# Eight more weight tiles split early and kept in DRAM, with their stores one plan entry later

## The chip, the cores and the metric

The kernel runs on one core of a Trainium2 chip. The metric is the device time of one execution, in microseconds (us). The core has a matrix engine (PE, with its weight loads as PEld), a vector engine (DVE), a scalar engine (ACT), a general engine (POOL) and a queue engine that issues the DMAs (SP). Each engine works through its own instructions in the order in which they were emitted; semaphores tie them to each other.

## The reference, cut to what matters

Two layers of a streaming encoder on a sequence of 512 rows with 1024 features. Layer 0 mixes with gated linear attention, layer 1 with chunked softmax attention; each layer then has a feed-forward block of width 4096. All weights are float32.

```python
def reference(x, c, w_ada, ...):
    c_act = jax.nn.silu(c)
    for i in range(DEPTH):                      # DEPTH = 2
        mods = jnp.split(c_act @ w_ada[i] + b_ada[i], 6, axis=-1)
        sh1, sc1, g1, sh2, sc2, g2 = [m[:, None, :] for m in mods]
        u = x * (1.0 + sc1) + sh1
        y = gla_mixer(u, ...) if i % 2 == 0 else chunk_attention(u, ...)
        x = layer_norm(ALPHA * x + (1.0 + g1) * y, ...)
        u = x * (1.0 + sc2) + sh2
        y = jnp.square(jax.nn.relu(u @ ff_w1[i])) @ ff_w2[i]
        x = layer_norm(ALPHA * x + (1.0 + g2) * y, ...)
    return x
```

`chunk_attention` has 16 heads; its input projections are `u @ att_w_in` (queries, keys, values) and its output projection is `o @ att_w_out`.

## The kernel before, in words

Activations lie feature by row, so a matmul's moving operand is a 128 x 512 tile of activations and its stationary operand a 128 x 128 block of weights. A **unit** is a weight tile of 128 x 1024 (eight such blocks) and makes one output tile of 128 x 512. To keep float32 accuracy every operand is split into a high part `hi` (a cast to float32r) and a low part `lo` (the value minus `hi`), and each block is multiplied three times, hi·hi, hi·lo and lo·hi (`mm3`). A unit is thus 24 matmuls.

Splitting a weight tile takes a load into a buffer of `rawp` (five buffers, `raw`), a cast on ACT (`A.copy`) and a subtraction on DVE (`lo_of`). The two results go into the pool `wp` (tags `whi` and `wlo`, four buffers each, for units used in order) or into two buffers of the pool `act` (26 buffers, shared with the activations; named `fhi` and `flo`).

What is loaded and split when is set by a list, `plan`, that is written before the program: `emit_unit` takes the next entry and emits its instructions. The kinds are `"w"` (load a unit and split it into `wp`), `"f"` and `"F"` (the same into `act`, for the four tiles that open a feed-forward block), `"a"` (one eighth of one modulation vector: load a tile, one DVE instruction on it), `"c"` (load a tile, split it into `act`, and store both parts to DRAM, "keep" it), and `"x"` and `"X"` (load a kept tile's two parts from DRAM straight into `wp` or `act`, with no cast and no subtraction). `next_w` hands out the next unit and then calls `fill`, which emits plan entries until three units are ready ahead. ACT and DVE run in the order of emission (`InOrder`); the DMAs are issued by SP in an order that the framework's scheduler chooses, and a DMA that waits holds up those behind it.

The feed-forward block of layer 0 (`add_mlp(0, ...)`) has 48 entries for units in its main loop, each with an `"a"` entry, and among them 18 `"c"` entries: the 14 query and key tiles of layer 1 from the second on (`kqk`), and tiles 0 to 3 of the output projection (`a_o`). Layer 1's attention takes them back as `"x"` and `"X"`. Its last four output-projection tiles are `"w"` entries, and the four tiles that open layer 1's feed-forward block are `"f"` and `"F"` entries; both are loaded and split while attention ends.

After attention comes `boundary(..., late=True)`: the output projection's tiles 0 to 3 over all rows (with the last heads' work between them, functions `t1` to `t5`), a matmul whose ACT copy gives `shift`, then `fill_f(4)`, then `sub` and `start_acc` (DVE and ACT) while PE does tiles 4 to 7 on the first half of the rows and tile 4 on the second half, then `stats1`, whose matmuls (`ones_c`) read the sums that DVE accumulates, and then the normalised tiles `un`, which PE takes half by half (`fg`). The boundary after layer 0's attention runs the same code from `stats1` on, `fg` included.

Of the kernel before, what the change touches and what calls it, by code (L numbers as in the profile page):

```python
# [9 lines left out]
F32 = mybir.dt.float32  # L10
# [49 lines left out]
def trunk(ctx, tc, xT, c, ada, cols, gk1, gk2, w_qk, w_v, w_g, w_go, a_qk, a_v, a_tab,  # L60
          a_win, a_o, f1, f2, out):
    nc = tc.nc
# [13 lines left out]
    def nm(s):  # L76
        uid[0] += 1
        return f"{s}{uid[0]}"
# [16 lines left out]
    def lo_of(eng, o, x, hi):  # L95
        return eng.tensor_tensor(out=o, in0=x, in1=hi.bitcast(F32), op=ALU.subtract)
# [35 lines left out]
    def ada_unit(l, t, k):  # L132
        raw = rawp.tile([P, D], F32, tag="raw", name=nm("raw"))
        nc.sync.dma_start(out=raw, in_=ada[l, t * 8 + k])
        i = t * 8 + k
        V.scalar_tensor_tensor(out=raw, in0=raw, scalar=1.0, in1=csil, op0=ALU.mult, op1=ALU.mult,
                               accum_out=mods[:, l, i:i + 1])
        if t == G2:
            tt(V, mods[:, l, i:i + 1], mods[:, l, i:i + 1], col[:, C_ADA + l * 48 + i:C_ADA + l * 48 + i + 1], ALU.add)
        elif k == KT - 1:  # L140
            m8 = mods[:, l, t * 8:t * 8 + 8]
            tt(V, m8, m8, col[:, C_ADA + l * 48 + t * 8:C_ADA + l * 48 + t * 8 + 8], ALU.add)
# [35 lines left out]
    plan = []  # L178
    state = {"pos": 0, "look": 0}
    ready_w, ready_f = [], []  # L180

    kept = {}

    def split_w(in_act):
        if in_act:
            return (act.tile([P, D], F32R, tag="act", name=nm("fhi")), act.tile([P, D], F32R, tag="act", name=nm("flo")))
        return (wp.tile([P, D], F32R, tag="whi", name=nm("whi")), wp.tile([P, D], F32R, tag="wlo", name=nm("wlo")))

    def emit_unit():
        kind, what = plan[state["pos"]]  # L190
        state["pos"] += 1
        if kind == "a":
            ada_unit(*what)
            return
        if kind in "xX":
            hi, lo = split_w(kind == "X")
            nc.sync.dma_start(out=hi.bitcast(F32), in_=kept[what][0])
            nc.sync.dma_start(out=lo.bitcast(F32), in_=kept[what][1])
            ready_w.append((hi, lo))
            return  # L200
        if kind == "c":
            key, src = what
            raw = rawp.tile([P, D], F32, tag="raw", name=nm("raw"))
            nc.sync.dma_start(out=raw, in_=src)
            hi, lo = split_w(True)
            A.copy(out=hi, in_=raw)
            lo_of(V, lo, raw, hi)
            kept[key] = [dram.tile([P, D], F32, name=f"{n}_{key[0]}{key[1]}") for n in ("khi", "klo")]
            nc.sync.dma_start(out=kept[key][0], in_=hi.bitcast(F32))
            nc.sync.dma_start(out=kept[key][1], in_=lo.bitcast(F32))  # L210
            return
        raw = rawp.tile([P, D], F32, tag="raw", name=nm("raw"))
        nc.sync.dma_start(out=raw, in_=what)
        hi, lo = split_w(kind in "fF")
        A.copy(out=hi, in_=raw)
        lo_of(V, lo, raw, hi)
        (ready_f if kind in "fF" else ready_w).append((hi, lo))

    def fill(n=None):
        n = state["look"] if n is None else n  # L220
        while len(ready_w) < n and state["pos"] < len(plan):
            emit_unit()

    def fill_f(n):
        while len(ready_f) < n:
            emit_unit()
# [13 lines left out]
    def add_units(units, adas=(), per=1, kind="w"):  # L240
        adas = list(adas)
        for u in units:
            plan.append((kind, u))
            for _ in range(per):
                if adas:
                    plan.append(("a", adas.pop(0)))

    def add_out(units, fgs, adas=(), early=False, pool=0):
        adas = list(adas)
        for i, u in enumerate(units):  # L250
            plan.append(("X", ("o", i)) if early and i < 4 else ("p" if i < pool else "w", u))
            if fgs and not early and 1 < i < 6:
                plan.append(("f", fgs[i - 2]))
            if adas and i < 4:
                plan.append(("a", adas.pop(0)))
        for a in adas:
            plan.append(("a", a))
        if early:
            plan.extend(("fF"[i // 2], u) for i, u in enumerate(fgs))

    def ada_list(l, *ts):
        return [(l, t, k) for t in ts for k in range(8)]

    add_units([w_v[k] for k in range(8)], ada_list(0, G1))
    add_units([w_g[k] for k in range(8)], ada_list(0, SC2, SH2), 2)
    fg1 = lambda l: [f1[l, m] for m in range(4)]
    add_out([w_go[k] for k in range(8)], fg1(0))

    def add_mlp(l, fgs, ad, keep=()):
        ad = list(ad)  # L270
        for m in range(4, 8):
            plan.append(("p" if m < 5 else "w", f1[l, m]))
        rest = [u for g in range(3) for u in [f2[l, g * 8 + m] for m in range(8)] + [f1[l, g * 8 + 8 + m] for m in range(8)]]
        keep = list(keep)
        for i, u in enumerate(rest):
            plan.append(("w", u))
            if ad:
                plan.append(("a", ad.pop(0)))
            if keep and i % 5 in (1, 3):
                plan.append(("c", keep.pop(0)))  # L280
        assert not ad and not keep
        add_out([f2[l, 24 + m] for m in range(8)], fgs)

    kqk = [q + p for p in range(1, 8) for q in (0, 8)]
    add_mlp(0, [a_v[k] for k in range(4)], ada_list(0, G2) + ada_list(1, SH1, SC1, G1, SC2, SH2),
            [(("q", i), a_qk[i]) for i in kqk] + [(("o", i), a_o[i]) for i in range(4)])
    add_units([a_v[k] for k in range(4, 8)])
    add_units([a_qk[0], a_qk[8]])
    for i in kqk:
        plan.append(("x", ("q", i)))  # L290
    add_out([a_o[k] for k in range(8)], fg1(1), early=True)
    add_mlp(1, [], ada_list(1, G2))

    def wk(w, k, n=P):
# [12 lines left out]
    def ln_cols(l, i, nxt):  # L307
        r = {}
        g = col[:, C_LNG + (l * 2 + i) * 8:C_LNG + (l * 2 + i) * 8 + 8]
        b = col[:, C_LNB + (l * 2 + i) * 8:C_LNB + (l * 2 + i) * 8 + 8]  # L310
        r["g"], r["b"] = g, b
        if nxt is not None:
            nl, sh, sc = nxt
            mS = mods[:, nl, sc * 8:sc * 8 + 8]
            mH = mods[:, nl, sh * 8:sh * 8 + 8]
            a1 = const.tile([P, 8], F32, name=nm("a1"))
            b1 = const.tile([P, 8], F32, name=nm("b1"))
            tt(V, a1, g, mS, ALU.mult)
            tt(V, b1, b, mS, ALU.mult)
            tt(V, b1, b1, mH, ALU.add)  # L320
            ag = const.tile([P, 8], F32, name=nm("ag"))
            ab = const.tile([P, 8], F32, name=nm("ab"))
            V.tensor_scalar(out=ag, in0=g, scalar1=ALPHA, scalar2=None, op0=ALU.mult)
            V.tensor_scalar(out=ab, in0=b, scalar1=ALPHA, scalar2=None, op0=ALU.mult)
            r.update(a=a1, b1=b1, ag=ag, ab=ab)
        return r
# [877 lines left out]
    def opener(es, n):  # L1204
        def f():
            if es is not None:
                es.close()
            e = ExitStack()
            cur["es"] = e
            cur["tmp"] = e.enter_context(tc.tile_pool(name=f"lnt{n}", bufs=1))  # L1210
            return cur["tmp"]
        return f
# [4 lines left out]
    o, ev, es = gla()  # L1217
    evac_h, run = mlp_fns()
    u = boundary(o, 0, G1, opener(es, 0), lambda: ln_cols(0, 0, (0, SH2, SC2)), evac_h, ev)
    hs = run(u, 0)  # L1220
    u = boundary(hs, 0, G2, open_v, lambda: ln_cols(0, 1, (1, SH1, SC1)), None, vfill=vfill)
    cur["es"].close()
    lnc1 = ln_cols(1, 0, (1, SH2, SC2))
    o, ev, es = att(u, cur["es_v"])
    evac_h, run = mlp_fns()
    u = boundary(o, 1, G1, opener(es, 1), lambda: lnc1, evac_h, ev, late=True)
# [55 lines left out]
```

## Time and profile before

| | |
|---|---|
| median of 3 runs (lowest to highest) | 1203.96 us (1203.43 to 1204.31) |
| the profiled execution | 1204.22 us, of which the profile's span is 1202.5 us |
| PE busy | 1175.6 us, 98% |
| PEld busy | 981.6 us, 82% |
| DVE busy | 825.9 us, 69% |
| ACT busy | 555.4 us, 46% |
| HBM read and written | 174.37 MB and 20.97 MB |

The profile is of one execution. Busy times are sums over the span, so an engine with a low share can still be the one that is waited for in a stage. PE's clock has two levels, 1.2 and 2.4 GHz; the profile gives it as a fraction of the higher one. A row of the time line gives a start, a length, the instruction group, and in square brackets how long the engine was idle before it and whom it waited for.

### The profile page before, as it was taken

To read this page: it belongs to the slowest core of one execution; us is meant where nothing else is said; L and a number is where in the kernel's file an instruction comes from. 1 tells how busy PE (TensorE), PEld (TensorE's weight loads), DVE (VectorE), ACT (ScalarE), POOL (GpSimd) and SP (SyncE) were. 2 spreads that over 40 slices of the span, in tenths; PEclk is the share of its full clock that TensorE was granted. 3 is DMA by queue.
4 is the path that set the end of the run, shared out by engine and by line. 5 is a ranking of instruction groups with operands and counts; after the bars stand their busy time and mean duration, and the time that the engine had idled before them with its cause. 6 is when DMAs were issued, how large, how long until landed. Compare 5 with 4: busy or idle time off the path is not lost.

```text
span 1202.5 us, 15104 instructions
## 1 busy us (share of the span) xinstructions
PE 1175.6 (98%) x5742; PEld 981.6 (82%) x5742; DVE 825.9 (69%) x1359; ACT 555.4 (46%) x870; POOL 51.5 (4%) x61
## 2 busy tenths in 40 slices
PE   9999999999999999999999999998999999999995
PEld 5888888898888888888888787787888888888885
DVE  6789589877676677657845889987774443443467
ACT  4565555484243343343546676554742322422324
POOL 2000000000000000000011233200000000000000
PEclk9999999999999999999999999998999999999998
DMA  9756534128889889854026431440263322232302
GB/s 349 256 181 220 193 105 150 44 85 298 311 307 339 295 306 318 306 180 158 12 92 230 158 114 53 149 141 1 73 218 130 98 98 97 94 105 88 105 1 71
DMA packets 58283, 196.34 MB, mean 163 GB/s; under 512 B 6561, under 2 KB 10913, under 8 KB 58210
## 3 DMA queue, kind: packets, MB, share of 16 engines
q1 hardware_dynamic: 58210, 195.37, 46.8%
q8 instruction: 45, 0.74, 0.2%
q14 instruction: 28, 0.23, 0.1%
HBM read 174.37 MB, written 20.97 MB: 162 GB/s over the span
## 4 chain that ended last, share of the span: by engine, by line
PE 77%; DVE 14%; ACT 4%; issue 2%; POOL 1%; DMA 1%; SPq 0%; DVEq 0%; ACTq 0%; POOLq 0%
PE ps L47 77%; DVE af L47 6%; DVE x L47 4%; ACT af L47 2%; DVE wlo L47 1%; ACT ar L47 1%; POOL mb L47 1%; DVE flo L47 1%; DMA hraw<-ada 1%; ACT u L47 0%; DVE d L47 0%; DVE t L47 0%; DVE ar L47 0%; DVE y L47 0%; DVE raw L47 0%
## 5 line engine op out<-in xcount | busy, mean ns | idle before, releaser
L47 PE MATMUL ps<-ar,whi 128*128 128x512 f32 (+1 forms) x2880 | 819.8, 373 | 0.6 <-ACT ar L47 0.4
L47 PEld LDWEIGHTS ps<-ar,whi 128*128 128x128 f32 x2880 | 525.1, 189 | 96.6 <-issue 2.2
L47 PE MATMUL ps<-ar,wlo 128*128 128x512 f32 (+1 forms) x1440 | 525.2, 371 | 0.1
L47 PEld LDWEIGHTS ps<-ar,wlo 128*128 128x128 f32 x1440 | 272.3, 189 | 46.9 <-DVE wlo L47 0.8
L47 ACT CAST whi<-raw 128x1024 fp32r<-128x1024 f32 (+1 forms) x169 | 169.4, 1010 | 199.4 <-PE ps L47 163.7
L47 DVE TENSOR_TENSOR wlo<-raw,whi 128x1024 fp32r<-128x1024 f32 x162 | 197.1, 1222 | 23.2 <-ACT whi L47 21.2
L47 DVE SCALAR_TENSOR_TENSOR x<-ps,mods,x 128x512 f32<-128x512 f32 (+1 forms) x96 | 63.2, 659 | 120.2 <-PE ps L47 119.9
L47 DVE TENSOR_TENSOR h<-r 128x512 f32<-128x512 f32 (+1 forms) x72 | 45.1, 632 | 79.2 <-ACT r L47 78.3
L47 ACT ACTIVATE r<-ps 128x512 f32<-128x512 f32 (+1 forms) x72 | 38.9, 546 | 126.9 <-PE ps L47 126.9
L47 DVE SCALAR_TENSOR_TENSOR raw<-raw,csil 128x1024 f32<-128x1024 f32 x80 | 96.8, 1217 | 0.0
L47 DVE TENSOR_TENSOR ar<-h,ar 128x512 fp32r<-128x512 f32 (+1 forms) x72 | 45.5, 632 | 39.6 <-ACT ar L47 38.5
L47 PE MATMUL ps<-ar,fhi 128*128 128x256 f32 (+1 forms) x320 | 68.9, 310 | 2.3 <-DVE ar L47 2.3
L47 ACT CAST ar<-h 128x512 fp32r<-128x512 f32 (+1 forms) x72 | 41.2, 573 | 50.4 <-DVE h L47 50.4
L47 PE MATMUL ps<-whi,ar 128*128 128x512 f32 x192 | 60.7, 390 | 0.0
L47 PEld LDWEIGHTS ps<-ar,fhi 128*128 128x128 f32 x320 | 52.0, 191 | 6.5 <-DVE ar L47 3.8
L47 PE MATMUL ps<-ar,flo 128*128 128x256 f32 (+1 forms) x160 | 48.7, 305 | 0.0
L47 ACT ACTIVATE af<-x 128x256 f32<-128x256 f32 (+1 forms) x48 | 23.0, 485 | 45.6 <-DVE x L47 42.4
L47 PEld LDWEIGHTS ps<-whi,ar 128*128 128x128 f32 x192 | 36.1, 188 | 7.6
L47 ACT CAST fhi<-raw 128x1024 fp32r<-128x1024 f32 x30 | 31.1, 1048 | 22.5 <-DMA raw<-a_qk 13.2
L47 DVE TENSOR_TENSOR ar<-f,ar 64x512 fp32r<-64x512 f32 x32 | 32.2, 1005 | 12.8 <-ACT ar L47 12.2
L47 ACT ACTIVATE ar<-x,b,a 128x256 fp32r<-128x256 f32 x48 | 28.5, 594 | 25.7 <-DVE x L47 25.7
L47 POOL PARTITION_ALL_REDUCE mb<-af x16 | 33.8, 2112 | 121.2 <-DVE af L47 121.2
(141 smaller groups left out, 1024.5 us busy)
## 6 DMA issues: line engine op xcount, KB each, us to landing
raw<-f SPq DMA_DIRECT2D x128, 512.0 KB, 4.3
raw<-ada SPq DMA_DIRECT2D x80, 512.0 KB, 4.8
hraw<-ada SPq DMA_DIRECT2D x16, 512.0 KB, 9.0
raw<-a_qk SPq DMA_DIRECT2D x16, 512.0 KB, 5.3
khi_q<-fhi SPq DMA_DIRECT2D x14, 512.0 KB, 2.9
klo_q<-flo SPq DMA_DIRECT2D x14, 512.0 KB, 4.7
whi<-khi_q SPq DMA_DIRECT2D x14, 512.0 KB, 3.3
wlo<-klo_q SPq DMA_DIRECT2D x14, 512.0 KB, 4.2
```

What stands on the lines that cost most here:

```text
L47: r = f(*a, **k)
```

## The change

Eight more tiles become `"c"` entries in layer 0's feed-forward block: tiles 4 to 7 of the output projection (`a_o`) and the four tiles that open layer 1's feed-forward block (`f1[1, 0..3]`). There are now 26; they come at every second of the 48 entries in the main loop (24), and the last two stand behind the first two entries of the block's closing list (`add_out`). In layer 1 output tiles 4 to 7 are `"x"` entries (loaded from DRAM into `wp`) and the four others are of a new kind `"Y"` (loaded from DRAM into `act`). The two stores of a `"c"` entry are emitted after the next entry of the plan.

```diff
@@ emit_unit
-    kept = {}
+    kept, stores = {}, []
...
     def emit_unit():
         kind, what = plan[state["pos"]]
         state["pos"] += 1
+        late, stores[:] = stores[:], []
+        try_unit(kind, what)
+        for to, hi, lo in late:
+            nc.sync.dma_start(out=to[0], in_=hi.bitcast(F32))
+            nc.sync.dma_start(out=to[1], in_=lo.bitcast(F32))
+
+    def try_unit(kind, what):
         if kind == "a":
             ada_unit(*what)
             return
-        if kind in "xX":
-            hi, lo = split_w(kind == "X")
+        if kind in "xXY":
+            hi, lo = split_w(kind != "x")
             nc.sync.dma_start(out=hi.bitcast(F32), in_=kept[what][0])
             nc.sync.dma_start(out=lo.bitcast(F32), in_=kept[what][1])
-            ready_w.append((hi, lo))
+            (ready_f if kind == "Y" else ready_w).append((hi, lo))
             return
         if kind == "c":
...
             kept[key] = [dram.tile([P, D], F32, name=f"{n}_{key[0]}{key[1]}") for n in ("khi", "klo")]
-            nc.sync.dma_start(out=kept[key][0], in_=hi.bitcast(F32))
-            nc.sync.dma_start(out=kept[key][1], in_=lo.bitcast(F32))
+            stores.append((kept[key], hi, lo))
             return
@@ add_out
-            plan.append(("X", ("o", i)) if early and i < 4 else ("p" if i < pool else "w", u))
+            plan.append(("X" if i < 4 else "x", ("o", i)) if early else ("w", u))
+            if keep:
+                plan.append(("c", keep.pop(0)))
...
         if early:
-            plan.extend(("fF"[i // 2], u) for i, u in enumerate(fgs))
+            plan.extend(("Y", ("f", i)) for i in range(4))
@@ add_mlp
-            if keep and i % 5 in (1, 3):
+            if keep and i % 2:
                 plan.append(("c", keep.pop(0)))
-        assert not ad and not keep
-        add_out([f2[l, 24 + m] for m in range(8)], fgs)
+        assert not ad
+        add_out([f2[l, 24 + m] for m in range(8)], fgs, keep=keep)
...
-            [(("q", i), a_qk[i]) for i in kqk] + [(("o", i), a_o[i]) for i in range(4)])
+            [(("q", i), a_qk[i]) for i in kqk] + [(("o", i), a_o[i]) for i in range(8)]
+            + [(("f", i), f1[1, i]) for i in range(4)])
```

On DVE at the end of layer 1's attention, before the change: the last subtraction for an output tile (`wlo`), the last heads' result (`ar`), the four residual updates (`x_94` to `x_97` from `ps`), four subtractions for the next block's tiles (`flo`), and the first two of the `sub` group.

```order
L47 TENSOR_TENSOR wlo_6807<-raw_6804,whi_6806 128x1024
L47 SCALAR_TENSOR_TENSOR ar_6810<-af_6783,col,ar_6810 128x512
L47 SCALAR_TENSOR_TENSOR x_94<-ps_6651,mods,x_94 128x512
L47 SCALAR_TENSOR_TENSOR x_95<-ps_6703,mods,x_95 128x512
L47 SCALAR_TENSOR_TENSOR x_96<-ps_6754,mods,x_96 128x512
L47 SCALAR_TENSOR_TENSOR x_97<-ps_6822,mods,x_97 128x512
L47 TENSOR_TENSOR flo_6881<-raw_6878,fhi_6880 128x1024
L47 TENSOR_TENSOR flo_6887<-raw_6884,fhi_6886 128x1024
L47 TENSOR_TENSOR flo_6893<-raw_6890,fhi_6892 128x1024
L47 TENSOR_TENSOR flo_6899<-raw_6896,fhi_6898 128x1024
L47 TENSOR_TENSOR x_98<-x_98,af_6612 128x512
L47 TENSOR_TENSOR x_94<-x_94,af_6612 128x512
```

The same place on DVE after the change:

```order
L47 SCALAR_TENSOR_TENSOR af_6861<-ps_6856,af_6861 64x512
L47 SCALAR_TENSOR_TENSOR ar_6882<-af_6861,col,ar_6882 128x512
L47 SCALAR_TENSOR_TENSOR x_94<-ps_6731,mods,x_94 128x512
L47 SCALAR_TENSOR_TENSOR x_95<-ps_6783,mods,x_95 128x512
L47 SCALAR_TENSOR_TENSOR x_96<-ps_6832,mods,x_96 128x512
L47 SCALAR_TENSOR_TENSOR x_97<-ps_6894,mods,x_97 128x512
L47 TENSOR_TENSOR x_98<-x_98,af_6692 128x512
L47 TENSOR_TENSOR x_94<-x_94,af_6692 128x512
```

The eight subtractions of that stage (four `wlo`, of which the last is shown, and four `flo`) are gone; nothing else moved. On ACT the eight casts beside them are gone in the same way.

On SP in the second half of layer 0's feed-forward block, before the change (`raw<-f` is a unit's load, `raw<-ada` a modulation tile's, `raw<-a_o` the load of a tile to keep, `khi_o` and `klo_o` the two stores):

```order
L209 DMA khi_o_4089<-fhi_4085 128x1024
L213 DMA raw_4129<-f 128x1024
L134 DMA raw_4161<-ada 128x1024
L210 DMA klo_o_4090<-flo_4086 128x1024
L213 DMA raw_4164<-f 128x1024
L134 DMA raw_4196<-ada 128x1024
L204 DMA raw_4199<-a_o 128x1024
L213 DMA raw_4209<-f 128x1024
L134 DMA raw_4241<-ada 128x1024
L209 DMA khi_o_4205<-fhi_4201 128x1024
L213 DMA raw_4244<-f 128x1024
```

The same queue after the change:

```order
L195 DMA khi_o_4165<-fhi_4161 128x1024
L196 DMA klo_o_4166<-flo_4162 128x1024
L219 DMA raw_4204<-f 128x1024
L134 DMA raw_4236<-ada 128x1024
L211 DMA raw_4239<-a_o 128x1024
L219 DMA raw_4247<-f 128x1024
L134 DMA raw_4281<-ada 128x1024
L195 DMA khi_o_4245<-fhi_4241 128x1024
L196 DMA klo_o_4246<-flo_4242 128x1024
L219 DMA raw_4284<-f 128x1024
L134 DMA raw_4322<-ada 128x1024
```

In both, a kept tile's load, a unit's load and a modulation load stand ahead of its first store; after the change the second store follows the first at once, and the next kept tile comes sooner.

On SP late in the attention, before the change (`af<-a_win` are two heads' bias windows at a time, `fhi` and `flo` from `khi_o` and `klo_o` are output tiles 0 and 1):

```order
L986 DMA af_6305<-a_win 128x256
L986 DMA af_6308<-a_win 128x256
L986 DMA af_6468<-a_win 128x256
L986 DMA af_6471<-a_win 128x256
L197 DMA fhi_6526<-khi_o_4009 128x1024
L198 DMA flo_6527<-klo_o_4010 128x1024
L197 DMA fhi_6591<-khi_o_4089 128x1024
L198 DMA flo_6592<-klo_o_4090 128x1024
L986 DMA af_6606<-a_win 128x256
L986 DMA af_6609<-a_win 128x256
```

The same place after the change, where `whi` and `wlo` are output tiles 6 and 7 (tiles 4 and 5 stand directly ahead of the first row):

```order
L995 DMA af_6548<-a_win 128x256
L995 DMA af_6551<-a_win 128x256
L204 DMA whi_6874<-khi_o_4245 128x1024
L205 DMA wlo_6875<-klo_o_4246 128x1024
L204 DMA fhi_6606<-khi_o_3733 128x1024
L205 DMA flo_6607<-klo_o_3734 128x1024
L204 DMA whi_6878<-khi_o_4331 128x1024
L205 DMA wlo_6879<-klo_o_4332 128x1024
L204 DMA fhi_6671<-khi_o_3826 128x1024
L205 DMA flo_6672<-klo_o_3827 128x1024
L995 DMA af_6686<-a_win 128x256
L995 DMA af_6689<-a_win 128x256
```

Output tiles 4 to 7 now stand among the bias windows and tiles 0 and 1, and each waits there for a buffer of `wp`; before, their raw tiles were loaded ahead of the attention.

## Rows read from the trace of the kernel before

**Rows 1.** The page: each engine's busy time and its share of the span.
```profile
PE 1175.6 (98%) x5742; PEld 981.6 (82%) x5742; DVE 825.9 (69%) x1359; ACT 555.4 (46%) x870; POOL 51.5 (4%) x61
```

**Rows 2.** Busy time by stage, with granted clock, DMA share and GB/s last.
```profile
core 0: us, PE busy (x) PEld busy (x) DVE busy (x) ACT busy (x) POOL busy (x), PEclk, DMA share, GB/s
9.00:36.00 27.00, 26.59 (x106) 19.73 (x105) 23.92 (x40) 13.62 (x22) 5.54 (x14) 1.00 1.03 406
255.30:516.40 261.10, 261.10 (x1154) 216.24 (x1153) 185.08 (x251) 104.00 (x131) 0.00 (x0) 1.00 0.84 298
277.30:320.30 43.00, 43.00 (x192) 35.61 (x191) 30.93 (x44) 13.16 (x14) 0.00 (x0) 1.00 0.93 336
814.70:820.10 5.40, 0.00 (x1) 0.00 (x1) 4.82 (x11) 1.25 (x3) 0.00 (x0) 0.93 0.00 0
820.10:825.80 5.70, 5.70 (x22) 5.34 (x23) 4.32 (x12) 1.63 (x4) 0.00 (x0) 0.50 0.00 0
```

**Rows 3.** Time line of PE at the end of layer 1's attention and its boundary.
```profile
757.09 1.45 PE L47 MATMUL ps<-ar,ar 128*128 128x512 f32 x8
...
794.92 0.39 PE L47 MATMUL ps<-ar,flo 128*128 128x512 f32 x1
795.14 0.39 PE L47 MATMUL ps<-ar,fhi 128*128 128x512 f32 x1
796.57 0.50 PE L47 MATMUL ps<-ar,fhi 128*128 128x512 f32 x1 [1.03 <-DVE ar L47]
...
814.34 0.28 PE L47 MATMUL ps<-ar,wlo 128*128 128x256 f32 x1
820.10 0.80 PE L47 MATMUL ps<-af,ones_c 128*128 128x256 f32 x1 [5.48 <-DVE af L47]
...
842.65 0.39 PE L47 MATMUL ps<-ar,fhi 128*128 128x256 f32 x1 [0.23 <-DVE ar L47]
```

**Rows 4.** Time line of DVE in the same stage.
```profile
766.85 1.52 DVE L47 SCALAR_TENSOR_TENSOR af<-ps,ng,af 128x256 f32<-128x256 f32 x4
...
792.35 3.50 DVE L47 TENSOR_TENSOR wlo<-raw,whi 128x1024 fp32r<-128x1024 f32 x3
795.76 0.75 DVE L47 SCALAR_TENSOR_TENSOR ar<-af,col,ar 128x512 fp32r<-128x512 f32 x1
...
800.29 0.75 DVE L47 SCALAR_TENSOR_TENSOR x<-ps,mods,x 128x512 f32<-128x512 f32 x1 [0.81 <-PE ps L47]
801.15 4.63 DVE L47 TENSOR_TENSOR flo<-raw,fhi 128x1024 fp32r<-128x1024 f32 x4
805.70 3.09 DVE L47 TENSOR_TENSOR x<-x,af 128x512 f32<-128x512 f32 x5
```

**Rows 5.** Time line of ACT in the same stage.
```profile
792.36 0.72 ACT L47 ACTIVATE ar<-af,col 128x512 fp32r<-128x512 f32 x1 [0.16 <-DVE af L47]
799.59 0.60 ACT L47 ACTIVATE af<-ps 128x512 f32<-128x512 f32 x1 [6.50 <-PE ps L47]
```

**Rows 6.** Time line of PE in the boundary after layer 0's attention.
```profile
219.81 0.99 PE L47 MATMUL ps<-af,ones_c 128*128 128x256 f32 x3 [1.30 <-DVE af L47]
240.52 0.38 PE L47 MATMUL ps<-ar,fhi 128*128 128x256 f32 x1 [0.23 <-DVE ar L47]
```

**Rows 7.** Groups by line, whole run: cast and subtraction of tiles split into `act`.
```profile
L47 DVE TENSOR_TENSOR flo<-raw,fhi 128x1024 fp32r<-128x1024 f32 x30 | 36.3, 1220 | 0.4 <-ACT fhi L47 0.3
L47 ACT CAST fhi<-raw 128x1024 fp32r<-128x1024 f32 x30 | 31.1, 1048 | 22.5 <-DMA raw<-a_qk 13.2 <-DMA raw<-a_o 6.9 <-DMA raw<-f 2.3
```

**Rows 8.** ACT's waits from 255 to 540: total us, times, longest.
```profile
ACT whi L47 <- PE ps L47: 43.4, 13, 6.6
ACT whi L47 <- DMA raw<-f: 18.1, 9, 5.1
```

**Rows 9.** SP's time line in the attention, and the landing of kept tiles (page).
```profile
756.60 1.01 SPq L986 DMA_DIRECT2D af<-a_win  x2
...
whi<-khi_q SPq DMA_DIRECT2D x14, 512.0 KB, 3.3
```

More of the change, by code (lines that the diff above doesn't have):

```diff
@@ L246, in add_units, with add_out @@
                     plan.append(("a", adas.pop(0)))
-    def add_out(units, fgs, adas=(), early=False, pool=0):
-        adas = list(adas)
+    def add_out(units, fgs, adas=(), early=False, keep=()):
+        adas, keep = list(adas), list(keep)
         for i, u in enumerate(units):
-            plan.append(("X", ("o", i)) if early and i < 4 else ("p" if i < pool else "w", u))
+            plan.append(("X" if i < 4 else "x", ("o", i)) if early else ("w", u))
+            if keep:
+                plan.append(("c", keep.pop(0)))
             if fgs and not early and 1 < i < 6:
```

## The prediction

> **What bounds the kernel now.** First the page: PE is busy for 98% of the span, the others for 69% or less [rows 1]. So little can be won, and only where PE stands still or runs at its lower clock, or lost where something new makes it wait.
>
> Then the busy time by stage, read against the two places that the change touches. In the 261.1 us of layer 0's feed-forward block in which all its 48 main entries are used (1154 matmuls, 24 a unit, so 48 units of 5.44 us) PE is busy for every microsecond. DVE is busy for 71% and ACT for 40% of it, and the DMA engines move 298 GB/s at a share of 0.84 [rows 2]. PE sets the pace there; everything else has slack, the DMAs least.
>
> At the end of layer 1's attention it is the other way round, and there I read the time lines of three engines side by side. PE stops twice: for 1.03 us before its matmul at 796.57, and for 5.48 us before the one at 820.10; both times it waits for DVE [rows 3]. DVE at those places is doing weight splits: three `wlo` (3.50 us) directly ahead of the `ar` that PE needs, and four `flo` (4.63 us) directly ahead of the `sub` group that begins the chain to the second wait [rows 4]. After the second stop PE's granted clock is 0.50 for 5.7 us, its level of 1.2 GHz; before it and after it is at 2.4 [rows 2].
>
> **The change part by part.**
>
> *Removed: four `wlo` and four `flo` on DVE, eight casts on ACT, at the end of attention.* The work is 8 x 1.22 us on DVE and 8 x 1.05 us on ACT [rows 7], but what counts is how much earlier PE goes on.
>
> First wait. The last result `ar` needs ACT's part, which starts at 792.36 and takes 0.72 us, so ends at 793.1 [rows 5]; DVE then adds 0.75 us [rows 4]: ready at 793.85 in place of 796.5. PE gets there after its matmul at 795.14. The two starts before are 0.22 us apart, so it would have gone on at 795.37 and did at 796.57 [rows 3]. The whole wait goes: **1.2 us**. All that follows on PE up to the next wait moves by that.
>
> Second wait. DVE's last residual update (800.29) waits for PE [rows 4], so it moves by 1.2 us as well. The four `flo` began at 801.15; the `sub` group now begins in their place, at 801.15 - 1.2 = 799.95. It also needs `shift`, an ACT copy at 799.59 for 0.60 us [rows 5], which waits for PE and so ends at 799.0. Hence `sub` begins at 799.95 in place of 805.70, **5.75 us** earlier, which contains the 1.2. From there to the `ones_c` matmul the chain is DVE's own work: that matmul comes at 820.10 - 5.75 = 814.35. PE's work before it ended at 814.62 [rows 3], now 813.4, so 0.9 us of idling is left. It is bounded below by nothing and above by what is left if ACT's squares, which DVE waits for inside that chain, come no earlier; they start from DVE's own results, so I expect them to follow.
>
> Clock. After a stop of 1.30 us at the same `ones_c` in layer 0's boundary [rows 6] the next matmuls ran at full length (three in 0.99 us, where at 820.10 the first alone shows 0.80). So I take a stop of 0.9 us to leave the clock alone. What that returns is read from the two boundaries, which run the same code from `ones_c` to the first long stretch of `fg`: 240.52 - 219.81 = 20.71 us at the full clock [rows 6] and 842.65 - 820.10 = 22.55 us here [rows 3]. **1.84 us**. Bounds: nothing, if the clock falls anyway, and half of the 5.7 us at 0.50, 2.85.
>
> *Added: eight more kept tiles in layer 0's block.* Eight casts (8.4 us) and eight subtractions (9.8 us) [rows 7] go where ACT has 157 us and DVE 76 us free in 261 [rows 2]. Cost 0; without that cover it would be 9.8. The DMAs are the real question. Per 48 units there were 48 + 48 + 18 x 3 = 150 transfers of 0.524 MB, and now 48 + 48 + 24 x 3 = 168: 12% more, 298 x 1.12 = 334 GB/s at a share of 0.94. The trace shows 336 GB/s held for 43 us in this very block, at 0.93, and 406 held for 27 us at the start of the program, with loads alone and many queued [rows 2]. So it fits, with little to spare. If it falls behind a little, there is a cushion: a buffer of `wp` comes free three units (16.3 us) before its new tile is used, and the split takes 1.05 + 1.22 us. The longest time that a cast waited for its load was 5.1 us, and mostly it waited for PE, 43.4 us against 18.1 [rows 8]: at the worst 16.3 - 2.3 - 5.1 = 8.9 us are left. I take **0**; the other end is under the rivals.
>
> The Trainium skill ("DMA: Bandwidth & Descriptors", Specifications) gives a limit of about 358 GB/s of HBM for one core. The 406 GB/s of rows 2 are above it, so the measurement decides. By the page the new rate would have 7% to spare instead of 18%; the sum would stay, and I would give starvation a chance of one in five instead of about one in seven.
>
> *Stores one entry later.* SP's order shows that the scheduler had already put the first store behind two later loads; the second moves little. What waits behind the stores on SP is the next unit's load. **0**, with a microsecond either way in the cushion.
>
> *Moved: the loads of attention's end.* Output tiles 4 to 7 and the four `f` tiles are 16 loads of 0.5 MB from DRAM in place of 8. On SP tile 7's pair waits for the buffer of the last key unit, which PE finishes at 757.1 [rows 3]; behind it stand tile 1 and the bias windows of heads 14 and 15, issued at 756.60 before [rows 9] and now at about 759. At 406 GB/s a load takes 1.3 us; landing was 3.3 us for the first [rows 9], so the windows land near 757.1 + 3.3 + 3 x 1.3 + 0.6 = 765. DVE reads the first of them at 766.85 [rows 4]: about 2 us to spare. The `Y` tiles are needed only in `fg`, some ten microseconds after `ones_c`; even if all eight were issued at 800 they would land by 800 + 8 x 1.3 + 2 = 812.4. **0**.
>
> **Sum.** 5.75 + 1.84 = 7.6 us off the profiled execution's 1204.22: 1196.6. That execution is 0.26 us above the median of the three runs, so 1196.4 against 1203.96; I say **1196.5**.
>
> **The rivals.**
>
> *The clock falls all the same.* For it: which stop makes it fall is shown by two cases only, 1.30 us and 5.48. Against: 0.9 is below the shorter. Time: 1204.2 - 5.75 = 1198.5. Chance 0.10.
>
> *The bias windows come late.* For it: SP now holds them behind four loads and PE. They would delay head 14's first DVE instruction, with all of DVE's work behind it busy. At 300 GB/s in place of 406 (1.75 us a load) they land at 767, and it costs nothing yet; it needs 4 us more latency to cost 2 to 3 us: about 1199. Chance 0.07.
>
> *The DMAs of layer 0's block fall behind: slower.* SP issues in order, and each pair of stores waits for a cast and a subtraction while loads wait behind them; with a keep at every second entry instead of two in five the dips come closer together. If the rate stays at 312 GB/s, between today's mean and the best 43 us, the block's 88.1 MB take 282.4 us, 21.3 more than PE's 261.1; the cushion hides 8.9, so PE stands for 12.4 us and the time is 1196.6 + 12.4 = 1209. It decides the sign from where the loss passes 7.6 us: 88.1 MB in 277.6 us, 317 GB/s. For it: the mean share must go to 0.94. Against: the 336 and the casts that wait for PE. Chance 0.13, about half of it beyond the point of no gain.
>
> **How the numbers follow.** The main case has 0.70: 1195 to 1198, its bounds being the clock's (5.75 + 2.85 off gives 1195.6, and up to 0.9 us of idling less). The first two rivals reach to 1199; a mild starvation of up to 4 us reaches 1201. The range 1194.8 to 1200.8 leaves out the worse half of the third rival and the fringes. A change of 0.2%, 2.4 us, is about what a measurement can tell here: faster means below 1201.5. Main case, the first two rivals and little of the third: 0.86 faster, 0.07 the same, 0.07 slower.
>
> **What the next profile would show.** If right: no PE wait of a microsecond before `shift`; one below 1.5 us before `ones_c`; granted clock 1.00 behind it; about 20.7 us from `ones_c` to `fg`'s long stretch; layer 0's block with PE always busy, at some 334 GB/s. Wrong: PE idle in layer 0's block, above all where a group's last activation passes behind a waiting cast on ACT; a wait of DVE for `a_win`; or a stop at `ones_c` as long as before, if something other than the splits holds DVE.

## The result, and the profile after

The median is 1196.7 us against 1203.93 us for the kernel before, measured beside it: a ratio of 0.9949, 95% interval [0.9939, 0.9958]. Five of the six executions lie between 1196.34 and 1197.65 us; one took 1202.08 us, and since it left no trace its cause is open. The profiled execution took 1196.6 us, 7.6 less than the profiled one of before.

The page after the change, to be read against [rows 1]:

```profile
span 1194.9 us, 15157 instructions
PE 1172.9 (98%) x5742; PEld 978.9 (82%) x5742; DVE 825.1 (69%) x1359; ACT 556.9 (47%) x870; POOL 51.6 (4%) x61
HBM read 182.76 MB, written 29.36 MB: 178 GB/s over the span
```

PE's busy time is 2.7 us shorter for the same 5742 matmuls (the clock: 2.6 of it lie between `ones_c` and `fg`'s long stretch), and its idle time, span less busy, went from 26.9 to 22.0 us. The two together are the 7.6. HBM moved 8.4 MB more each way, eight tiles of two parts.

PE's time line at the end of layer 1's attention, to be read against [rows 3]:

```profile
796.91 0.62 PE L47 MATMUL ps<-ar,fhi 128*128 128x512 f32 x2
797.36 0.40 PE L47 MATMUL ps<-ar,flo 128*128 128x512 f32 x1
797.59 0.59 PE L47 MATMUL ps<-x,ones_h 128*128 128x512 f32 x1
...
814.42 1.21 PE L47 MATMUL ps<-af,ones_c 128*128 128x256 f32 x4 [0.73 <-DVE af L47]
...
835.07 0.39 PE L47 MATMUL ps<-ar,fhi 128*128 128x256 f32 x1 [0.22 <-DVE ar L47]
```

The wait before `shift`'s matmul (`ones_h`) is gone, the one before `ones_c` is 0.73 us in place of 5.48, and from there to `fg`'s long stretch it takes 20.65 us in place of 22.55. DVE in the same stage, against [rows 4]:

```profile
793.43 0.75 DVE L47 SCALAR_TENSOR_TENSOR ar<-af,col,ar 128x512 fp32r<-128x512 f32 x1 [0.79 <-ACT ar L47]
...
799.36 0.75 DVE L47 SCALAR_TENSOR_TENSOR x<-ps,mods,x 128x512 f32<-128x512 f32 x1 [0.81 <-PE ps L47]
800.02 3.09 DVE L47 TENSOR_TENSOR x<-x,af 128x512 f32<-128x512 f32 x5
```

The `sub` group follows the last residual update at once. Then the busy time by stage (columns as in [rows 2]; the last two of each row are DMA share and GB/s): layer 0's block, the 38 us behind it, both together, and what follows `ones_c`.

```profile
255.30:516.40 261.10, 261.10 (x1155) 216.25 (x1154) 189.26 (x256) 110.45 (x136) 0.00 (x0) 1.00 0.86 322
516.40:554.50 38.10, 38.10 (x170) 31.55 (x169) 25.16 (x35) 19.27 (x23) 1.11 (x4) 1.00 0.88 320
255.30:554.50 299.20, 299.20 (x1323) 247.80 (x1322) 214.43 (x290) 129.73 (x159) 1.11 (x4) 1.00 0.86 322
814.42:825.80 11.38, 11.38 (x91) 11.12 (x92) 9.66 (x26) 5.72 (x13) 0.00 (x0) 1.00 0.00 0
```

PE loses nothing in the block, and its clock stays up behind `ones_c`. But the DMAs moved 322 GB/s there and not the 334 forecast, and part of the rest came late: 320 GB/s in the 38 us after, where before the change it was 155. Of the 13 transfers more that SP issues in those 38 us, six are the two kept tiles of the closing list and seven the block's own. The block in two parts, before the change and then after it:

```profile
255.30:275.00 19.70, 19.70 (x89) 16.29 (x88) 14.56 (x23) 15.47 (x27) 0.00 (x0) 1.00 0.45 135
275.00:516.40 241.40, 241.40 (x1067) 199.95 (x1066) 170.52 (x229) 88.54 (x105) 0.00 (x0) 1.00 0.87 312
```

```profile
255.30:275.00 19.70, 19.70 (x90) 16.36 (x89) 14.49 (x24) 15.45 (x27) 0.00 (x0) 1.00 0.41 134
275.00:516.40 241.40, 241.40 (x1067) 199.89 (x1066) 174.77 (x233) 95.01 (x110) 0.00 (x0) 1.00 0.90 338
```

By 211 us SP has issued five unit loads, as many as `rawp` has buffers, and then waits for DVE to be done with them; so in the first 19.7 us of the block the rate is the same low one in both kernels. Behind it the rate rose from 312 to 338 GB/s: the mean of 322 holds a start that the added tiles couldn't use. ACT's waits from 255 to 540 us show how close the supply now is, against [rows 8]:

```profile
ACT whi L47 <- DMA raw<-f: 86.0, 35, 6.2
```

The casts now wait for their loads, 35 times in place of 9; the waits of `whi` for PE, 43.4 us before, are gone from the list. PE is still the one that ends last, but the stage is fed just in time.

### The profile page after: what moved, and what is told of

The parts are those of the page before. It is cut to its first block, busy times and chain, and to the rows that moved or that the text cites. A ratio compares the mean times of both kernels' runs of the same rounds, so it can differ in the third digit from the quotient of the medians.

```text
span 1194.9 us, 15157 instructions
## 1 busy us (share of the span) xinstructions
PE 1172.9 (98%) x5742; PEld 978.9 (82%) x5742; DVE 825.1 (69%) x1359; ACT 556.9 (47%) x870; POOL 51.6 (4%) x61
## 4 chain that ended last, share of the span: by engine, by line
PE 81%; DVE 12%; ACT 4%; issue 2%; DMA 1%; POOL 0%; SPq 0%; ACTq 0%; DVEq 0%; POOLq 0%
PE ps L47 81%; DVE x L47 4%; DVE af L47 4%; ACT af L47 1%; ACT ar L47 1%; DVE wlo L47 1%; ACT u L47 1%; DMA hraw<-ada 1%; DVE d L47 1%; DVE t L47 0%; DVE y L47 0%; DVE ar L47 0%; DVE raw L47 0%; POOL mb L47 0%; ACT L47 0%
## 5 line engine op out<-in xcount | busy, mean ns | idle before, releaser
L47 ACT CAST whi<-raw 128x1024 fp32r<-128x1024 f32 (+1 forms) x165 | 165.5, 1010 | 217.6 <-PE ps L47 116.3
L47 DVE TENSOR_TENSOR wlo<-raw,whi 128x1024 fp32r<-128x1024 f32 x158 | 192.5, 1222 | 67.8 <-ACT whi L47 64.9
L47 ACT ACTIVATE r<-ps 128x512 f32<-128x512 f32 (+1 forms) x72 | 39.0, 547 | 88.3 <-PE ps L47 88.1
L47 ACT CAST fhi<-raw 128x1024 fp32r<-128x1024 f32 x34 | 35.7, 1051 | 28.3 <-DMA raw<-a_qk 17.5
L47 DVE TENSOR_TENSOR flo<-raw,fhi 128x1024 fp32r<-128x1024 f32 x34 | 41.5, 1221 | 3.5 <-ACT fhi L47 3.5
```

Source lines behind the costliest of these rows:

```text
L47: r = f(*a, **k)
```

## The experiments

The theory: what stands on DVE ahead of `ar` and ahead of `sub` sets two stops of PE; the longer one also costs clock; the extra traffic is hidden by what lies ahead in the queues. The rivals: the gain is spread over all eight tiles; it comes from the stores; the clock isn't its cause; the traffic is nowhere near a limit.

**Only the output tiles.** Tiles 4 to 7 kept, the four `f` tiles split as before.

```diff
-            [(("q", i), a_qk[i]) for i in kqk] + [(("o", i), a_o[i]) for i in range(8)]
-            + [(("f", i), f1[1, i]) for i in range(4)])
+            [(("q", i), a_qk[i]) for i in kqk] + [(("o", i), a_o[i]) for i in range(8)])
...
-            plan.extend(("Y", ("f", i)) for i in range(4))
+            plan.extend(("fF"[i // 2], u) for i, u in enumerate(fgs))
```

> Only output tiles 4 to 7 are kept; the four tiles that open the next feed-forward block are split at the end of attention as before the change. Theory (a stop at ones_c is priced by what stands ahead of sub): the wait before shift goes, 1.2 us, but four flo still stand ahead of sub, so the stop at ones_c stays at about 5.5 us and the clock behind it at 0.50: 1203.9 - 1.2 = 1202.7 us. Rival (each moved tile is worth the same, 0.9 us): 1203.9 - 3.6 = 1200.3 us, with a shorter stop.

1202.92 us, ratio 0.9992 [0.9983, 1.0001]. DVE's time line:

```profile
799.02 0.75 DVE L47 SCALAR_TENSOR_TENSOR x<-ps,mods,x 128x512 f32<-128x512 f32 x1 [0.81 <-PE ps L47]
799.89 4.63 DVE L47 TENSOR_TENSOR flo<-raw,fhi 128x1024 fp32r<-128x1024 f32 x4
804.44 1.89 DVE L47 TENSOR_TENSOR x<-x,af 128x512 f32<-128x512 f32 x3
```

And PE's:

```profile
818.84 2.07 PE L47 MATMUL ps<-af,ones_c 128*128 128x256 f32 x4 [5.48 <-DVE af L47]
...
840.34 0.39 PE L47 MATMUL ps<-ar,fhi 128*128 128x256 f32 x1 [0.23 <-DVE ar L47]
```

As the theory has it: the first wait goes, but DVE begins `sub` that much behind the same four `flo`, and PE, earlier too, waits the same 5.48 us. Half of the tiles bring 1.1 us. One thing differs: from `ones_c` to the long stretch it takes 21.50 us, where before the change the same stop was followed by 22.55, and the clock in the 5.7 us behind the stop is 0.71 and not the 0.50 expected.

**Only the feed-forward tiles.** The four `f` tiles kept, tiles 4 to 7 split as before.

```diff
-            [(("q", i), a_qk[i]) for i in kqk] + [(("o", i), a_o[i]) for i in range(8)]
+            [(("q", i), a_qk[i]) for i in kqk] + [(("o", i), a_o[i]) for i in range(4)]
...
-            plan.append(("X" if i < 4 else "x", ("o", i)) if early else ("w", u))
+            plan.append(("X", ("o", i)) if early and i < 4 else ("w", u))
```

> Only the four tiles that open the next feed-forward block are kept; output tiles 4 to 7 are split in wp during attention as before the change. Theory: the wait of about 1 us before shift is there again, sub comes 4.55 us earlier than before the change, the stop at ones_c is about 1 us and the clock behind it stays at 1.00: 1203.9 - 4.55 - 1.84 = 1197.5 us. Rival (each moved tile is worth the same): 1200.3 us. Rival (the clock falls at a stop near 1 us here): 1199.4 us.

1197.86 us, ratio 0.9948 [0.9935, 0.9962], and the steadiest of all: five executions from 1197.80 to 1197.99. PE's time line:

```profile
796.90 0.50 PE L47 MATMUL ps<-ar,fhi 128*128 128x512 f32 x1 [1.01 <-DVE ar L47]
...
815.68 1.21 PE L47 MATMUL ps<-af,ones_c 128*128 128x256 f32 x4 [0.74 <-DVE af L47]
...
836.33 0.38 PE L47 MATMUL ps<-ar,fhi 128*128 128x256 f32 x1 [0.23 <-DVE ar L47]
```

The first wait is back, the second short, the clock up: 20.65 us from `ones_c` on. The four `f` tiles bring 6.1 us. With the 1.1 of the other four that makes 7.2, the whole.

**Stores at once, and stores later alone.** First the change with the stores emitted in the entry that splits; then the kernel before with only the stores one entry later (the new `emit_unit` and `try_unit`, 18 kept tiles).

```diff
-            stores.append((kept[key], hi, lo))
+            nc.sync.dma_start(out=kept[key][0], in_=hi.bitcast(F32))
+            nc.sync.dma_start(out=kept[key][1], in_=lo.bitcast(F32))
```

> The change with the two stores of a kept tile emitted at once, in the entry that splits it, as before the change. Theory (the scheduler already puts the stores behind later loads, and the weight tiles of layer 0's block are about 9 us ahead of PE): 1196.7 us, the same within 0.5, with PE busy throughout 255 to 516 us. Rival (a store that waits for its split holds up the next unit's load on SP and the denser keeps have no slack left): PE stands in layer 0's block, 1200 us or more.

> The kernel before the change with only the stores emitted one plan entry later; 18 kept tiles as before. Theory: no change, 1203.9 us, since the queue has slack and the scheduler had already put other loads ahead of the stores. Rival (the stores held up loads of the block): nothing to win there either, since PE is busy throughout that block; a loss of up to 1 us if a load is late.

1197.18 us (1196.71 to 1197.66), ratio 0.9943 [0.993, 0.9955]; and 1203.70 us, ratio 0.9998 [0.9989, 1.0007]. The later stores are worth nothing by themselves, and at most half a microsecond within the change, which these runs can't tell from nothing. The profiles show why: in both pairs SP issues the DMAs from 250 to 560 us in the same order (187 of them with the change, 163 before it). The scheduler makes the same queue of either program, so neither run moved a store on the queue.

**The stop alone.** The change with k extra subtractions on DVE ahead of `sub`, k = 2, 4 and 7. They write a buffer that is written again before it is read.

```diff
             fill_f(4)
+            for _ in range(k):
+                tt(V, shs[:, 1, :], xs[4], xs[4], ALU.subtract)
```

> The change with two extra DVE subtractions of 128x512 (0.62 us each, into a buffer that is written again before it is read) directly ahead of sub: the stop at ones_c grows from 1.2 to about 2.45 us. If the clock holds: +1.24, 1197.9 us. If it falls at this length: +1.24 + 1.84, 1199.8 us, and a granted clock near 0.50 for the next 5 to 6 us.

> The change with four extra DVE subtractions of 128x512 directly ahead of sub: stop at ones_c about 3.7 us. If the clock holds: +2.5, 1199.2 us. If it falls: +2.5 + 1.84, 1201.0 us.

> The change with seven extra DVE subtractions of 128x512 directly ahead of sub: stop at ones_c about 5.55 us, as long as before the change (5.48), with all else as after the change. Theory (the 22.55 us from ones_c to the next block's long stretch, against 20.7, are the clock's doing): the clock is at 0.50 behind the stop, +4.3 + 1.84, 1202.9 us. Rival (the 1.84 us came from the splits and loads at that place, not from the stop): +4.3, 1201.0 us, with 20.7 us from ones_c to the long stretch.

Measured 1199.05 (ratio 0.9959 [0.9947, 0.9972]), 1200.86 (0.9977 [0.9968, 0.9986]) and 1202.49 us (0.9991 [0.9983, 1.0]). With two, the median lies between the forecasts for a clock that holds (1197.9) and for one that falls (1199.8), and the profile decides: the clock is 1.00. Its execution took 1198.63 us, 2.03 more than the change's; 1.53 are the longer stop and 0.5 stand ahead of this stage. With four, the median is near the forecast for a clock that falls (1201.0), but in the profiled execution, 1200.17 us, the fall cost 0.7 us and not 1.84. With seven, the 5.7 us behind `ones_c` by the view of stretches, and PE's time line:

```profile
819.33:825.03 5.70, 5.70 (x24) 5.34 (x25) 4.32 (x12) 1.64 (x4) 0.00 (x0) 0.54 0.00 0
```

```profile
819.33 2.07 PE L47 MATMUL ps<-af,ones_c 128*128 128x256 f32 x4 [5.89 <-DVE af L47]
...
841.52 0.39 PE L47 MATMUL ps<-ar,fhi 128*128 128x256 f32 x1 [0.23 <-DVE ar L47]
```

Seven kernels side by side, from the same two rows and the same stretch of each:

| kernel | stop at `ones_c`, us | clock in the 5.7 us behind | to the long stretch, us |
|---|---|---|---|
| the change | 0.73 | 1.00 | 20.65 |
| `f` tiles only | 0.74 | 1.00 | 20.65 |
| two extra | 2.26 | 1.00 | 20.65 |
| four extra | 3.71 | 0.70 | 21.36 |
| output tiles only | 5.48 | 0.71 | 21.50 |
| before | 5.48 | 0.50 | 22.55 |
| seven extra | 5.89 | 0.54 | 22.19 |

No `flo`, no extra load, only a longer stop, and the clock falls: the rival that put the 1.84 us on the splits is out (by it 20.7 us with seven, measured 22.19). The clock held at 2.26 us of idling and fell at 3.71; what it cost then was 0.7 to 1.9 us, and two stops of the same 5.48 us differ by 1.05. In these two the clock was at another level already within the stop: 0.93 over its 5.48 us before the change, 0.68 with the output tiles only, so there more of the low stretch passed while PE stood. Why it began earlier there isn't shown. Each extra subtraction lengthened the stop by 0.74 us, not 0.62: (5.89 - 0.73) / 7.

**More traffic in layer 0's block.** Six, and then three, further tiles kept there that nobody uses (32 and 29 in place of 26); the list of kept tiles grows by as many.

```diff
-            if keep and i % 2:
+            if keep and i % 3:
```

```diff
-            if keep and i % 2:
+            if keep and (i % 2 or i in (12, 24, 36)):
```

> The change with six further tiles loaded, split and stored in layer 0's block that nobody uses: kept tiles at two of three entries (32) in place of one of two; layer 1 unchanged. The block's 48 units then need 192 transfers of 0.524 MB in place of 168, 101 MB, 385 GB/s at PE's pace. Theory (the queues hold some 340 GB/s with loads and stores mixed and the cushion is about 9 us): the block takes 101/0.340 = 296 us, 35 over 261, PE stands for some 26 us: about 1223 us (1239 at 322 GB/s, 1206 at 360). Rival (the rate goes on rising with demand, as the 406 GB/s at the program's start): 1197 us, PE busy throughout.

> The change with three further tiles loaded, split and stored in the middle of layer 0's block that nobody uses (29 in place of 26). With 32, the queues moved about 329 GB/s and 40 us were lost. Theory (that rate is the limit, and the change is at its edge): 92.8 MB at 329 GB/s take 282 us, 21 more than PE's 261; with 10 to 18 us hidden by loads ahead, PE stands for 3 to 11 us and its clock falls at some of the stops: 1200 to 1211 us. Rival (32 overran a threshold that 29 doesn't reach): 1196.7 us, PE busy throughout.

1236.91 us (ratio 1.0276 [1.0262, 1.029]) and 1214.39 us (1.0083 [1.007, 1.0097]). The block and the 38 us behind it by the view of stretches, with 32 kept tiles:

```profile
255.30:554.50 299.20, 278.73 (x1192) 225.49 (x1192) 197.87 (x262) 115.23 (x142) 0.00 (x0) 0.97 0.87 319
```

With 29:

```profile
255.30:554.50 299.20, 291.55 (x1269) 239.57 (x1267) 208.43 (x278) 123.56 (x154) 0.00 (x0) 0.99 0.87 322
```

Three demands, one rate: 322, 322 and 319 GB/s with 26, 29 and 32 tiles, and from 275.00 to 516.40 us 338, 335 and 331. What is asked beyond it is paid in time. How it reaches PE is seen with 29 tiles, on ACT and on PE:

```profile
457.19 1.05 ACT L47 CAST fhi<-raw 128x1024 fp32r<-128x1024 f32 x1 [0.89 <-DMA raw<-a_o]
458.49 1.04 ACT L47 CAST whi<-raw 128x1024 fp32r<-128x1024 f32 x1 [0.25 <-DMA raw<-f]
459.44 0.59 ACT L47 ACTIVATE r<-ps 128x512 f32<-128x512 f32 x1
461.43 0.62 ACT L47 CAST ar<-h 128x512 fp32r<-128x512 f32 x1 [1.40 <-DVE h L47]
```

```profile
457.55 0.39 PE L47 MATMUL ps<-ar,wlo 128*128 128x512 f32 x1
462.10 1.52 PE L47 MATMUL ps<-ar,whi 128*128 128x512 f32 x2 [4.16 <-ACT ar L47]
```

Weights are not what PE waits for. A group's last activation passes ACT twice, as `r` and, after a product on DVE (`h`), as `ar`. Its `r` stands on ACT directly behind two casts that waited for their loads, and the next group needs its `ar` at once. PE's waits for it from 255 to 620 us (total, times, longest):

```profile
PE ps L47 <- ACT ar L47: 10.1, 3, 4.5
```

The matmuls behind them run at the lower clock (0.79 granted on the mean from 459 to 475 us), so the price is more than the idling.

**Bytes or tiles?** The 29 tiles again, with the eight modulation loads of `G1` of layer 1 taken out of the 48 entries (four into the closing list, four behind it).

```diff
-            if ad:
+            if ad and (i < 8 or i % 5 != 2):
                 plan.append(("a", ad.pop(0)))
...
-        add_out([f2[l, 24 + m] for m in range(8)], fgs, keep=keep)
+        add_out([f2[l, 24 + m] for m in range(8)], fgs, tail, keep=keep)
```

> The 29 kept tiles that cost 17.7 us, with the eight modulation loads of G1 of layer 1 taken out of the block's 48 main entries: four now stand in the block's closing list and four at the tiles behind it. Casts, subtractions and stores of the kept tiles are as in that run; the 48 entries need 169 transfers in place of 177, nearly the 168 of the change. Theory (bytes in the block decide: the queues hold about 329 GB/s there whatever they carry): PE stands little or not at all in the block, 1196.7 to 1200 us. Rival (it is the kept tiles themselves, whose stores wait on the in-order queue and whose casts stand ahead of the group's activation): 1212 us or more, with stops that end with ACT's ar as before.

1202.43 us (1201.64 to 1206.27), ratio 0.9994 [0.9985, 1.0003]. Of the 17.7 us that the three tiles cost, 12.0 are back, with every cast, subtraction and store of them in place. PE's waits for ACT's `ar` went from 10.1 to 4.7 us:

```profile
PE ps L47 <- ACT ar L47: 4.7, 2, 3.2
```

So it is mostly how much is asked of the queue, as the theory has it, though it ended 2.4 us above the theory's upper end. All these transfers are of one size, so bytes and their number aren't told apart. Up to the block's end this kernel still issues five transfers more than the change (one in the 48 entries, four in the closing list): 2.6 MB, 8.1 us at 322 GB/s, of which 5.7 show.

**Order alone.** With only the `f` tiles kept, the last heads' result ahead of the splits.

```diff
-            fill(5)
             fin3(7)
+            fill(5)
```

> Only the four tiles that open the next feed-forward block are kept, output tiles 4 to 7 are split as before the change, but the last heads' result (fin3(7)) is emitted ahead of fill(5), so that ar stands ahead of the three wlo on DVE and ACT. Theory (the wait before shift is a matter of DVE's order alone): that wait goes as in the change and the rest is as with the four tiles kept, 1197.86 - 1.2 = 1196.7 us. Rival (the splits are only moved, and the residual updates or the next weight tiles are late in their place): 1197.9 us.

1197.57 us, ratio 0.9947 [0.9934, 0.9959]: at most 0.3 of the 1.2 us, and by the two intervals not told from nothing. PE's time line and DVE's:

```profile
799.06 1.12 PE L47 MATMUL ps<-x,ones_h 128*128 128x512 f32 x2 [1.03 <-DVE x L47]
```

```profile
793.78 0.75 DVE L47 SCALAR_TENSOR_TENSOR ar<-af,col,ar 128x512 fp32r<-128x512 f32 x1 [0.79 <-ACT ar L47]
794.73 3.50 DVE L47 TENSOR_TENSOR wlo<-raw,whi 128x1024 fp32r<-128x1024 f32 x3 [0.19 <-ACT whi L47]
798.26 2.07 DVE L47 SCALAR_TENSOR_TENSOR x<-ps,mods,x 128x512 f32<-128x512 f32 x3
```

The rival was right: `ar` comes in time, but the residual updates now stand behind the three `wlo`, and `shift`'s matmul waits for them, 1.03 us where `ar` cost 1.01. The wait moved to the next matmul that needs DVE.

**The splits on another engine.** The kernel before with that order and the four `flo` on POOL.

```diff
-        lo_of(V, lo, raw, hi)
+        lo_of(G if kind == "F" else V, lo, raw, hi)
...
-            plan.extend(("fF"[i // 2], u) for i, u in enumerate(fgs))
+            plan.extend(("F", u) for u in fgs)
```

> The kernel before the change (18 kept tiles) with two edits: fin3(7) ahead of fill(5), and the four flo subtractions on POOL in place of DVE. No further tile is kept. Theory (only what stands on DVE ahead of ar and of sub counts, and POOL is idle there): both gains without the extra DRAM traffic, 1196.7 us, stop at ones_c about 1 us, clock 1.00. Rival (POOL's subtractions slow DVE's while both run, by as much as they take off it): sub later or longer, stop of 3 us or more, 1199 to 1203 us.

1207.00 us, ratio 1.0027 [1.0017, 1.0036]: slower than before, worse than the rival. DVE and POOL:

```profile
800.41 11.94 DVE L47 TENSOR_TENSOR x<-x,af 128x512 f32<-128x512 f32 x5
812.27 0.68 DVE L47 TENSOR_TENSOR af<-x,x 128x512 f32<-128x512 f32 x1
```

```profile
800.66 11.14 POOL L47 TENSOR_TENSOR flo<-raw,fhi 128x1024 fp32r<-128x1024 f32 x4 [22.95 <-DMA raw<-f]
```

While POOL subtracts for 11.14 us, DVE's five subtractions, elsewhere 3.09 us, take 11.94; behind it DVE is at its usual 0.68 again. PE's stop at `ones_c` is 9.57 us.

## Why the prediction came out

**The two stops: right.** Forecast and measured: `sub` at 799.95 and 800.02, `ones_c` at 814.35 and 814.42, the idling left 0.9 and 0.73 us. The two runs with one half of the tiles give the terms apart, 1.1 and 6.1 us. ACT's squares did follow, which was the bound that had stayed open.

**The clock: right here, but no fixed price.** 20.7 us forecast, 20.65 measured. The extra subtractions show that the stop alone brings the clock down. The 1.84 us were one execution's price; other stops of the same order cost 0.7 to 1.9.

**Stores and moved loads at 0: right** for the stores, and for a plainer reason than the prediction gave: their later place in the plan leaves SP's order as it was. For the bias windows the evidence is the trace alone: they were issued at 759.26 us, where about 759 was forecast, and DVE's time line has no wait for `a_win`.

**Added keeps at 0: right in the sum, wrong in its reason.** The step that failed is "So it fits, with little to spare", with 334 GB/s at a share of 0.94. The queues gave 322 at 0.86, and neither 92.8 nor 100.7 MB drew more from them than the 88.1 MB of the 48 entries. Of these 168 transfers SP had issued 160 by 516.40 us; before the change it had issued all 150. At 322 the 88.1 MB take 273.6 us, 12.5 more than PE's 261.1. By the prediction's own cushion of 8.9 us PE should have stood for 3.6; it didn't, so the cushion too was mis-sized, at 12.5 us at least. The two errors cancelled. The third rival's mechanism was real and its signature, the group's last activation behind a waiting cast, was named correctly; its break-even, 317 GB/s, lay 5 GB/s from the rate that came, and its chance of 0.13 was low for that margin.

What the step overlooked is in its own 298: that mean holds 19.7 us at 135 GB/s in which SP waits for DVE, and the step scaled them up with the rest. They stayed at 134. For a mean of 334 the other 241.4 us would have had to run at about 350 GB/s (an estimate from these rows); they ran at 338, and with 29 and 32 tiles at 335 and 331. So the 336 GB/s of the 43 us were no sign of room. They were about all that this queue gave, and the 406 were loads alone.

The Trainium skill ("DMA: Bandwidth & Descriptors", Specifications) has about 358 GB/s of HBM for one core. No run here held that over the block: the measured 331 to 338 from 275 us on are below it, as the 406 at the program's start are above it.

**What is left of the cushion: next to nothing.** Three tiles more are nine transfers, 4.7 MB, 14.7 us at 322 GB/s, and cost 17.7. Six tiles more are 18 transfers by the block's end and 24 within the 48 entries (the cadence differs), 29 to 39 us, and cost 40.2. So beyond the change the bytes are paid in full. The kernel with only the `f` tiles kept asks 162 transfers, 84.9 MB or 264 us at that rate, gives away 1.1 us, and its times lie within 0.2 us. Its casts wait for their loads as often as the change's (84.1 us in 36 waits), so these waits alone don't mark the edge. Whether the change's one execution at 1202.08 is a stop in that block isn't shown.

Open: why no more than 331 to 338 GB/s came at a share of 0.90. A rival to a limit of the DMAs is SP's in-order queue. Its waits in the block before the first store of a kept tile, before the change and after:

```profile
SPq L209 <- ACT fhi L47: 50.0, 18, 4.9
```

```profile
SPq L195 <- ACT fhi L47: 111.5, 23, 6.8
```

SP now stands there for 111.5 of 261.1 us, and no load behind it is issued meanwhile. Around the end of one of these waits, from 415.00 to 419.60 us, the DMA share is 0.68 (237 GB/s); in the 2.5 us behind all 23 of them it is 0.70 on the mean. The run with the stores at once has the same order on SP and the same waits (113.5 us in 23), so it can't decide. Whether stores that don't hold up the loads would raise the rate isn't shown.

## What to carry to other kernels

Price a removed instruction by the wait behind it: four splits ahead of `sub` were worth 6.1 us, four others 1.1, though the work was the same. Work moved into a stage that "has slack" is paid from a stock: before a mean rate is scaled up, look for the part of the stage that can't take more, and find the edge by adding a little more of the same, for beyond it every transfer costs. When an edit changes the order of emission, compare the order on the queue first. Before work is put on an idle engine or merely later, look at what it shares with the busy one and at what stands next in the queue.

## What the runs showed of the hardware

- PE's granted clock held at 2.4 GHz behind stops of 0.73 and 2.26 us and fell to 1.2 GHz behind or shortly after one of 3.71; two stops of 5.48 us were followed by mean clocks of 0.50 and 0.71 over the next 5.7 us.
- Loads and stores mixed, issued by one in-order queue, ran at 338, 335 and 331 GB/s over 241.4 us with 88, 93 and 101 MB asked for in the block, at a DMA share of 0.90.
- POOL and DVE didn't work side by side on tensors in SBUF: five DVE subtractions went from 3.09 to 11.94 us under 11.14 us of POOL subtractions (2.8 us each, against 1.2 on DVE). The Trainium skill ("GPSIMD Engine Reference", Specifications) says that POOL shares its SBUF interfaces with VectorE, with contention for DVE instructions that have two SBUF inputs; these are such, and the trace agrees.
